# Later unit loads, an earlier parameter step and later state pairs in a one-core recurrent decoder step

## The chip, the core and the metric

The kernel runs on one core of one Trainium2 chip. The metric is device time of one execution in microseconds (us), and the time of a kernel is the median of several executions. TensorE (PE), VectorE (DVE), ScalarE (ACT), GpSimd (POOL) and SyncE (SP) each work through their own queue in order; they wait for one another through semaphores. SP does nothing here but issue transfers from the chip's main memory. ACT and POOL issue a few as well.

## The reference

The program is one inference step of a decoder layer for 256 prompt tokens and 8 samples of 4 tokens (288 columns in all), with width 2048, in float32. What is computed:

- A modulation: `mod = silu(c) @ w_ada + b_ada`, six vectors of 2048 for each of nine conditions. They shift and scale the normed input of both halves of the layer and gate their results.
- `proj = xn @ w_in`, split into the inputs of three branches and three merge gates.
- Branch 1, a linear recurrence (RG-LRU): a causal convolution of width 4, then `r` and `i` as sigmoids of block-diagonal products, `log_a = 8 * r * log_sigmoid(lam)`, `a = exp(log_a)`, `u = sqrt(1 - exp(2 log_a)) * i * x`, and the scan `h = a*h + u`.
- Branch 2, gated linear attention (GLA), and branch 3, mLSTM, both with matrix states that are read, updated and written for each sample.
- `merged = sum over branches of sigmoid(gate) * (y @ w_br)`, then `x + gt1 * (merged @ w_out)`, and an MLP with squared ReLU, a last norm, and all new states.

## The kernel before

**Tiles.** Activations lie feature by feature: 128 features on the partitions, 288 columns along the free axis. Every large product runs through `stream_` (line 183). A block of weights is 512 output columns wide. It comes in granules: a granule is one raw tile of 128 x 1024 (two times 128 rows of the weight matrix), fetched by SP at line 155, halved into a high part on ACT (`hi`, line 164) and a low part on DVE (`lo`, line 171), and used by 24 matmuls of 288 columns (lines 197 to 199: hi times the activations' high and low parts, lo times their high part). There are three buffers each for raw, hi and lo. Four PSUM tiles `mm` hold one block; a block's evacuation by ACT or DVE must free them before the next block uses them.

**Units.** The modulation's weights are cut into units of 1 MB (`first` and `ada`). `load_one` (line 411) has SP issue a unit's transfer (lines 378, 380 and 391), and `visit` (line 416) has PE run its small matmuls (line 341). Units have buffers of their own, taken in turn from the list in `slots`: a number is a large slot that is free at that time, `None` is the ring tile `ag`, `"st"` is a pair of small tiles. A unit's transfer can only be issued once the visit of the buffer's last unit is over.

**Order.** SP's instructions are put out in the order in which the program emits them (SP is scheduled by hand). The other engines' orders are made by a planner, which simulates the program and picks by priority; `issue_after` puts an instruction behind another one on the same engine. `run` (line 252) goes through a block granule by granule. After each granule it does one step of the pattern that `every` set: `L` loads a unit, `V` visits all units that are loaded, `W` and `N` are a small product's load and work, and a dot does nothing. Then it lets each generator in `side` (the recurrence, GLA, mLSTM) take one step, up to its next `yield`, with high priority and behind the granule's last matmul, hi and lo on their engines. Because raw tiles have three buffers, SP is some granules ahead of PE in its order; when it comes to a load whose buffer is not free, all fetches behind it wait too.

**Stages.** The first product runs in stages 0 to 5 as parts of the modulation become known. Stage 5 (line 764) has 12 granules and the pattern `L L WL L . VN . L L . V .`. After its tenth granule the recurrence `lru()` (line 684) starts beside it. Then come two gate blocks of 8 granules (line 811), whose evacuations are a tanh on ACT (line 807) and a product on DVE (line 808), and the merge of branch 1 (line 1132), in which four times 8 granules of gate weights alternate with 4 of `wbl`. `finish(lru_)` (line 1147) drains what is left of the recurrence before the first 4. The later merges run beside GLA and mLSTM.

**The recurrence.** `lru()` first runs `conv` (line 652): transfers and a group of small operations on POOL, then, for each of 8 feature tiles, one ACT and three DVE operations, with six yields. Then it computes its parameters from `lam` (lines 694 to 713: 128 x 8 values, two ACT and some twenty DVE operations), yields, and runs ten steps in which PE makes two small products per tile (line 728) and ACT makes two tanh, a tanh and an Exp of the tile two steps back (lines 722 to 724). Four square roots on ACT follow (line 731), four groups of products on DVE (735 to 737), the scans (747) and the split into high and low parts (523 and 524).

**mLSTM.** The 16 state tiles of 0.5 MB are loaded on POOL (line 1444), read by PE in pairs (line 1461), updated on DVE and stored on POOL (line 1483). `when(n)` (line 1508) gives the step of pair n; the loads and later steps are tied to it.

Of the kernel before, what the change touches and what calls it, by code (L numbers as in the profile page):

```python
# [10 lines left out]
AF = mybir.ActivationFunctionType  # L11
# [42 lines left out]
def trunk(ctx, tc, io):  # L54
    nc = tc.nc
    PSUM = bass.MemoryType.PSUM
    V, S, G, T, Q = nc.vector, nc.scalar, nc.gpsimd, nc.tensor, nc.sync
# [19 lines left out]
    def slot(i, dt=F32):  # L77
        return big.tile([P, 8, N], dt, tag=f"s{i}", name=nm(f"s{i}"))
# [22 lines left out]
    def Pm(n):  # L101
        a, w = POFF[n]
        return par[:, a:a + w]
# [144 lines left out]
    def every(p, skip=0):  # L248

        pace.update(every=p.split(), n=-skip)  # L250
# [37 lines left out]
    a, w = COFF["eye"]  # L288
# [17 lines left out]
    slots = {"ids": (None,), "n": 1}  # L306
# [275 lines left out]
    qk, vv, lx = slot(8), slot(9), slot(2)  # L582
# [66 lines left out]
    pace.update(pins=pace["adds"][-2:-1])  # L649
    run(stream(win, B_LRU + 1, act1, 2, None, keep=kept))  # L650

    def conv(x, y, w, b, state, cout, scr):

        w = w.rearrange("p (k j) -> p k j", k=8)
        f = flat(scr)
        xp = f[:, 0:448].rearrange("p (k b j) -> p k b j", k=8, b=NB)
        acc = f[:, 448:704].rearrange("p (k b t) -> p k b t", k=8, b=NB)
        tmp = f[:, 704:960].rearrange("p (k b t) -> p k b t", k=8, b=NB)
        co = f[:, 960:1176].rearrange("p (k j) -> p k j", k=8)
        G.dma_start(f[:, 1176:1368], io[state])  # L660
        G.tensor_copy(xp[:, :, :, 3:7], smp(x))
        G.tensor_copy(xp[:, :, :, 0:3], f[:, 1176:1368].rearrange("p (k b j) -> p k b j", k=8, b=NB))
        bc = [P, 8, NB, TS]
        for j in range(4):
            wj = w[:, :, j:j + 1].unsqueeze(3).to_broadcast(bc)
            if j == 0:
                G.tensor_tensor(out=acc, in0=xp[:, :, :, 0:4], in1=wj, op=ALU.mult)
                G.tensor_tensor(out=acc, in0=acc, in1=b.unsqueeze(2).unsqueeze(3).to_broadcast(bc), op=ALU.add)
            else:
                G.tensor_tensor(out=tmp, in0=xp[:, :, :, j:j + 4], in1=wj, op=ALU.mult)  # L670
                G.tensor_tensor(out=smp(y) if j == 3 else acc, in0=acc, in1=tmp, op=ALU.add)
        G.tensor_copy(co[:, :, 0:3], x[:, :, NP - 3:NP])
        G.tensor_copy(co[:, :, 3:27].rearrange("p k (b j) -> p k b j", b=NB), xp[:, :, :, 4:7])
        G.dma_start(io[cout], co)
        for m in range(8):
            S.activation(y[:, m, 0:NP], x[:, m, 0:NP], AF.Identity, bias=b[:, m:m + 1], scale=w[:, m, 3:4])
            for j in (2, 1, 0):
                s = 3 - j
                V.scalar_tensor_tensor(y[:, m, s:NP], x[:, m, 0:NP - s], w[:, m, j:j + 1], y[:, m, s:NP], ALU.mult, ALU.add)
            if m not in (0, 3):  # L680
                yield


    def lru():
        wax = slot(3)
        wa = flat(wax)[:, 0:1024].rearrange("p (n d) -> p n d", n=8)
        wx = flat(wax)[:, 1024:2048].rearrange("p (n d) -> p n d", n=8)
        G.dma_start(flat(wax)[:, 0:2048], io["lruw"])
        uc = slot(4)
        yield from conv(lx, uc, Pm("lcw"), Pm("lcb"), "lst", "o_lconv", slot(1))  # L690

        lam = Pm("lam")
        e, s, z, a_ = (sc([P, 8], f"lam{i}", 1) for i in range(4))
        S.activation(e, lam, AF.Abs)
        S.activation(e, e, AF.Exp, scale=-1.0)
        V.tensor_scalar(s, e, 2.0, None, ALU.add)
        V.reciprocal(s, s)
        V.tensor_tensor(out=s, in0=s, in1=e, op=ALU.mult)
        V.tensor_tensor(out=z, in0=s, in1=s, op=ALU.mult)
        V.memset(a_, 1.0 / 19)  # L700
        for n in range(8, -1, -1):
            V.tensor_tensor(out=a_, in0=a_, in1=z, op=ALU.mult)
            V.tensor_scalar(a_, a_, 1.0 / (2 * n + 1), None, ALU.add)
        V.tensor_tensor(out=a_, in0=a_, in1=s, op=ALU.mult)
        ls = sc([P, 8], "lam4", 1)
        V.tensor_scalar(ls, lam, 0.0, None, ALU.min)
        V.scalar_tensor_tensor(ls, a_, -2.0, ls, ALU.mult, ALU.add)
        ls2, ls4 = sc([P, 8], "lam5", 1), sc([P, 8], "lam6", 1)
        V.tensor_scalar(ls2, ls, 2.0, None, ALU.mult)
        V.tensor_scalar(ls4, ls, 4.0, None, ALU.mult)  # L710
        hb = sc([P, 2, 8], "hb", 1)
        V.tensor_scalar(hb[:, 0, :], Pm("ba"), 0.5, None, ALU.mult)
        V.tensor_scalar(hb[:, 1, :], Pm("bx"), 0.5, None, ALU.mult)
        yield
        thr, thi, tt = slot(5), slot(0), slot(1)
        aa = thr
        ps = {}
        for n in range(8 + 2):
            if n >= 2:
                i = n - 2  # L720
                for j, t in ((0, thr), (1, thi)):
                    S.activation(t[:, i, :], ps.pop((i, j))[:, :N], AF.Tanh, bias=hb[:, j, i:i + 1], scale=0.5)
                S.activation(tt[:, i, :], thr[:, i, :], AF.Tanh, bias=ls2[:, i:i + 1], scale=ls2[:, i:i + 1])
                S.activation(aa[:, i, :], thr[:, i, :], AF.Exp, bias=ls4[:, i:i + 1], scale=ls4[:, i:i + 1])
            if n < 8:
                for j, w in ((0, wa), (1, wx)):
                    ps[n, j] = misc()
                    T.matmul(ps[n, j][:, :N], w[:, n, :], uc[:, n, :], start=True, stop=True)  # L728
            yield
        for h in range(4):  # L730
            S.activation(tt[:, 2 * h:2 * h + 2], tt[:, 2 * h:2 * h + 2], AF.Sqrt, scale=-0.25)
        yield
        for h in range(4):
            r = slice(2 * h, 2 * h + 2)
            V.scalar_tensor_tensor(thi[:, r], thi[:, r], 1.0, uc[:, r], ALU.add, ALU.mult)
            V.tensor_tensor(out=thi[:, r], in0=thi[:, r], in1=tt[:, r], op=ALU.mult)
            V.scalar_tensor_tensor(thi[:, r], aa[:, r], 1.0, thi[:, r], ALU.add, ALU.mult)
            yield
        st = sc([P, 8, NB], "lh0", 1)
        V.tensor_tensor(out=st, in0=aa[:, :, NP:N:TS], in1=Pm("h0").rearrange("p (k b) -> p k b", k=8), op=ALU.mult)  # L740
        V.tensor_tensor(out=thi[:, :, NP:N:TS], in0=thi[:, :, NP:N:TS], in1=st, op=ALU.add)
        V.memset(aa[:, :, NP:N:TS], 0.0)
        V.memset(aa[:, :, 0:1], 0.0)
        hh = slot(3)
        for h in range(8):
            r = slice(h * N, (h + 1) * N)
            V.tensor_tensor_scan(flat(hh)[:, r], flat(aa)[:, r], flat(thi)[:, r], 0.0, ALU.mult, ALU.add)
            if h % 2:
                yield
        ho = sc([P, 8, 9], "lho", 1)  # L750
        G.tensor_copy(ho[:, :, 0:1], hh[:, :, NP - 1:NP])
        G.tensor_copy(ho[:, :, 1:9], hh[:, :, NP + 3:N:TS])
        G.dma_start(io["o_lh"], ho)
        ylru.extend([slot(0, F32R), slot(1, F32R)])
        for h in range(4):
            r = slice(2 * h, 2 * h + 2)
            split(ylru[0][:, r], ylru[1][:, r], hh[:, r])
            yield
# [2 lines left out]

    a, w = COFF["eye"]
    for i, turn, p in ((2, (5, 4, 0, 1, 2, 3), "F2LL F1FL 2FLL 1 2 ."), (3, (3, 2, 1, 0, 4, 5), "L L . L LV . L L . LLV . ."),
                       (4, (5, 4, 0, 1, 2, 3), "L L . L LV . L L . LLV . ."), (5, (3, 4, 5, 0, 1, 2), "L L WL L . VN . L L . V .")):
        k0, k1, _ = STAGES[i]
        if i == 5:
            slots.update(ids=(6, 7, 3, None), n=0)
        pace.update(hpins=pace["copies"][-1:])
        lead = begin(i, p)
        if i < 5:  # L770
# [37 lines left out]
            V.scalar_tensor_tensor(sg[:, base + m, :], th, 1.0, p, ALU.add, ALU.mult)  # L808
        return f

    every("L L L L . V . .")
    slots.update(ids=("st", None, 6, 7), n=0)
    run(stream(win, B_GATE, act1, KT, gate_silu(0)))
    run(stream(win, B_GATE + 1, act1, KT, gate_silu(4)))

# [316 lines left out]
    def merge(br, y, w):  # L1132
        for b in range(4):
            if br == 0 and b == 2:
                visit()
                slots.update(ids=(None,), n=0)
                every("L . V . . .")
            if br == 0:
                gt = acc[b // 2][:, 4 * (b % 2):4 * (b % 2) + 4, :]
            elif br == 1:  # L1140
# [28 lines left out]
            run(stream(w, b, lambda k: (y[0][:, k, :], y[1][:, k, :]), 8, ev))  # L1169

    slots.update(ids=(None, 7), n=0)
    every("L L . V . .")
    merge(0, ylru, io["wbl"])
    visit()
    every("")
# [85 lines left out]
    def mlstm():  # L1261
# [34 lines left out]
        for t in range(2):  # L1296
            for q in range(2):
                p = misc()
                for i in range(4):
                    n = 4 * q + i  # L1300
# [6 lines left out]
        for h in range(4):  # L1307
            for e in range(2):
                n = 2 * h + e
# [4 lines left out]
        for h in range(4):  # L1314
            for e in range(2):
                n = 2 * h + e
# [3 lines left out]
        for t in range(2):  # L1320
            for q in range(2):
                p = misc()
                for i in range(4):
                    n = 4 * q + i
                    T.matmul(p[:, i * P:(i + 1) * P], mc[:, n, t * P:(t + 1) * P], bdk[:, n * P:(n + 1) * P], start=True, stop=True)
                for i in range(2):
                    h = 2 * q + i
# [30 lines left out]
        for h in range(4):  # L1358
            for e in range(2):
                n = 2 * h + e  # L1360
# [145 lines left out]
            at.setdefault(s, []).append(lambda: f(*a))  # L1506

        def when(n):
            return 5 + n // 2 * 3 + (n >= 10)

        do(0, part, kp, ks, 0, K_LO)
        do(0, part, vp, vs[:, 0:256], 0, V_LO)
# [53 lines left out]

    visit()
    slots.update(ids=(None, "st", 5), n=0)
    every("L L L . V . .", skip=6)
    merge(2, yml, io["wbm"])  # L1570


# [250 lines left out]
```

## Time and profile before

| | us |
|---|---|
| runs, median of 3 (lowest to highest) | 1957.53 (1956.1 to 1958.71) |
| profiled execution, its own time | 1953.31 |
| span of the profiled execution | 1951.5 |
| PE busy with matmuls | 1923.9 |
| DVE busy | 1035.4 |
| ACT busy | 809.7 |
| POOL busy | 233.8 |

The span goes from the first to the last instruction; 1.81 us of the execution lie around it. PE's busy time counts a stretch as busy when at least one matmul is under way; matmuls overlap, so what counts for the rate is how far apart they start. `A <- B` after an engine and a line means that A waited for B, with the sum of the waits, how many there were, and the longest.

### The profile page before, as it was taken

To read this page: it belongs to the slowest core of one execution; us is meant where nothing else is said; L and a number is where in the kernel's file an instruction comes from. 1 tells how busy PE (TensorE), PEld (TensorE's weight loads), DVE (VectorE), ACT (ScalarE), POOL (GpSimd) and SP (SyncE) were. 2 spreads that over 40 slices of the span, in tenths; PEclk is the share of its full clock that TensorE was granted. 3 is DMA by queue.
4 is the path that set the end of the run, shared out by engine and by line. 5 is a ranking of instruction groups with operands and counts; after the bars stand their busy time and mean duration, and the time that the engine had idled before them with its cause. 6 is when DMAs were issued, how large, how long until landed. Compare 5 with 4: busy or idle time off the path is not lost.

```text
span 1951.5 us, 35926 instructions
## 1 busy us (share of the span) xinstructions
PE 1923.9 (99%) x15068; PEld 1827.7 (94%) x15068; DVE 1035.4 (53%) x1595; ACT 809.7 (41%) x1130; POOL 233.8 (12%) x334
## 2 busy tenths in 40 slices
PE   8999999999999999999999999999999999999997
PEld 6898889999999998899999899999999999999997
DVE  6665746535673456654454564445454445454565
ACT  4333474443554353433333454443334333343433
POOL 0000100011042112000012330000000000000101
PEclk9999999999999999999999999999999999999999
DMA  9997766557443468876788464455444444444452
GB/s 393 380 353 258 270 233 233 195 186 266 156 164 110 141 214 306 279 261 252 281 318 320 171 216 153 159 178 169 163 162 163 162 162 164 167 166 172 160 173 107
DMA packets 110065, 416.42 MB, mean 213 GB/s; under 512 B 11632, under 2 KB 11808, under 8 KB 106192
## 3 DMA queue, kind: packets, MB, share of 16 engines
q1 hardware_dynamic: 100800, 381.55, 54.6%
q0 software_dynamic: 8096, 29.19, 4.2%
q10 hardware_dynamic: 1008, 3.39, 0.5%
q8 instruction: 118, 1.93, 0.4%
q14 instruction: 43, 0.35, 0.1%
HBM read 397.27 MB, written 16.81 MB: 212 GB/s over the span
## 4 chain that ended last, share of the span: by engine, by line
PE 95%; DMA 2%; DVE 1%; issue 1%; ACT 0%; POOL 0%; SPq 0%; DVEq 0%; ACTq 0%; POOLq 0%
PE mm L197 28%; PE mm L199 28%; PE mm L198 28%; PE pa L341 4%; DMA raw<-win 1%; DMA s<-wad 1%; PE px L728 0%; DMA s<-mC 0%; PE px L1006 0%; DMA s<-x 0%; PE px L1477 0%; PE pi L1461 0%; PE px L1391 0%; PE px L128 0%; DVE lo L171 0%
## 5 line engine op out<-in xcount | busy, mean ns | idle before, releaser
L171 DVE TENSOR_TENSOR lo<-raw,hi 128x1024 fp32r<-128x1024 f32 x448 | 549.0, 1228 | 563.4 <-ACT hi L164 543.7
L164 ACT ACTIVATE hi<-raw 128x1024 fp32r<-128x1024 f32 x444 | 470.5, 1060 | 794.0 <-PE mm L198 602.0
L197 PE MATMUL mm<-xh,hi 128*128 128x288 f32 x2528 | 744.6, 299 | 4.4 <-DVE s L808 2.0
L198 PE MATMUL mm<-xl,hi 128*128 128x288 f32 x2528 | 741.3, 296 | 0.0
L199 PE MATMUL mm<-xh,lo 128*128 128x288 f32 x2528 | 725.6, 295 | 0.9 <-DVE lo L171 0.8
L197 PEld LDWEIGHTS mm<-xh,hi 128*128 128x128 f32 x2528 | 471.7, 188 | 25.0 <-issue 11.8
L197 PE MATMUL mm<-s,hi 128*128 128x288 f32 x1664 | 490.7, 297 | 0.0
L198 PE MATMUL mm<-s,hi 128*128 128x288 f32 x1664 | 488.2, 295 | 0.0
L199 PE MATMUL mm<-s,lo 128*128 128x288 f32 x1664 | 476.5, 295 | 0.4 <-DVE lo L171 0.4
L198 PEld LDWEIGHTS mm<-xl,hi 128*128 128x128 f32 x2528 | 474.2, 188 | 1.3
L199 PEld LDWEIGHTS mm<-xh,lo 128*128 128x128 f32 x2528 | 469.0, 188 | 3.1 <-DVE lo L171 1.6
L197 PEld LDWEIGHTS mm<-s,hi 128*128 128x128 f32 x1664 | 311.9, 188 | 5.5 <-issue 4.2
L198 PEld LDWEIGHTS mm<-s,hi 128*128 128x128 f32 x1664 | 312.5, 188 | 0.3
L199 PEld LDWEIGHTS mm<-s,lo 128*128 128x128 f32 x1664 | 308.3, 188 | 0.8 <-DVE lo L171 0.7
L171 DVE TENSOR_TENSOR lo<-s,hi 128x1024 fp32r<-128x1024 f32 x80 | 98.0, 1225 | 113.4 <-ACT hi L164 113.4
L164 ACT ACTIVATE hi<-s 128x1024 fp32r<-128x1024 f32 x80 | 84.9, 1061 | 142.4 <-PE mm L198 141.7
L1651 POOL TENSOR_TENSOR t<-t 128x288 f32<-128x288 f32 x64 | 60.2, 951 | 639.2 <-ACT t L1650 639.2
L603 DVE TENSOR_TENSOR s<-s,mm 128x288 f32<-128x288 f32 x92 | 39.6, 450 | 43.4 <-PE mm L199 42.4
L1667 DVE TENSOR_TENSOR s<-s,mm 128x288 f32<-128x288 f32 x96 | 40.3, 450 | 33.9 <-PE mm L199 32.6
L1163 POOL TENSOR_TENSOR s<-s,t 128x288 f32<-128x288 f32 x32 | 33.5, 1074 | 192.6 <-DVE t L1162 192.6
L341 PE MATMUL pa<-s,silc 128*32 128x64 f32 (+3 forms) x832 | 51.2, 373 | 0.7 <-DMA s<-wad 0.6
L524 DVE TENSOR_TENSOR s<-t,s 128x288 fp32r<-128x288 f32 x64 | 33.8, 568 | 15.5 <-ACT s L523 15.5
(404 smaller groups left out, 1152.7 us busy)
## 6 DMA issues: line engine op xcount, KB each, us to landing
raw<-win SPq DMA_DIRECT2D x188, 512.0 KB, 4.8
raw<-wf SPq DMA_DIRECT2D x176, 512.0 KB, 4.1
s<-wf SPq DMA_DIRECT2D x80, 512.0 KB, 3.6
s<-wada SPq DMA_DIRECT2D x26, 1024.0 KB, 9.5
s<-wad SPq DMA_DIRECT2D x24, 1024.0 KB, 10.2
ag<-wada SPq DMA_DIRECT2D x22, 1024.0 KB, 5.6
raw<-wout SPq DMA_DIRECT2D x32, 512.0 KB, 5.6
st<-wada SPq DMA_DIRECT2D x20, 512.0 KB, 6.6
```

The source lines that it names most:

```text
L164: pace["hi"] = S.activation(hi, raw, AF.Copy)
L171: pace["lo"] = V.tensor_tensor(out=lo[:, r], in0=raw[:, r], in1=hi[:, r].bitcast(F32), op=ALU.subtract)
L197: T.matmul(pss[m][:, :N], hi[:, kk, ms], xh, start=k == k0 and not take, stop=False)
L198: T.matmul(pss[m][:, :N], hi[:, kk, ms], xl, start=False, stop=False)
L199: pace["last"] = T.matmul(pss[m][:, :N], lo[:, kk, ms], xh, start=False, stop=k == kt - 1 and keep is None)
L341: pace["prod"] = T.matmul(ps[32 * j:32 * j + 32, h * w // 4:(h + 1) * w // 4], silu_c(k), v[:, j], start=k == 0 and h == 0, stop=k == KT - ...
L524: pace["mod"] = V.tensor_tensor(out=dst_l[:, r], in0=src[:, r], in1=dst_h[:, r].bitcast(F32), op=ALU.subtract)
L603: pace["adds"].append(V.tensor_tensor(out=dst[:, base + m, :], in0=dst[:, base + m, :], in1=p, op=ALU.add))
L1163: G.tensor_tensor(out=a, in0=a, in1=t, op=ALU.add)
L1651: G.tensor_tensor(out=r, in0=r, in1=r, op=ALU.mult)
L1667: V.tensor_tensor(out=a, in0=a, in1=p, op=ALU.add)
```

## The change

- `conv` gets a flag; with it, it yields once after its operations on POOL and before the first of the eight tiles.
- `lru()` computes its parameters before `conv`, with a yield after the reciprocal, and calls `conv` with the flag. It has one yield more than before ahead of its first gate product.
- The four square roots are issued behind the last Exp on ACT.
- Stage 5 loads its last two units at steps 10 and 11 and not at 7 and 8, into slots 5 and 6 and not 6 and 7, and visits them at step 11 and not 10.
- The gate blocks, both parts of the merge of branch 1 and the merge of branch 3 load one step later; their visits stay. The gate blocks use slot 7 before slot 6.
- The mLSTM pairs 10, 12 and 14 run one step later, with what is tied to them.

```diff
-    def conv(x, y, w, b, state, cout, scr):
+    def conv(x, y, w, b, state, cout, scr, apart=False):
...
         G.dma_start(io[cout], co)
+        if apart:
+            yield
         for m in range(8):
...
         uc = slot(4)
-        yield from conv(lx, uc, Pm("lcw"), Pm("lcb"), "lst", "o_lconv", slot(1))
-
         lam = Pm("lam")
...
         V.reciprocal(s, s)
+        yield
         V.tensor_tensor(out=s, in0=s, in1=e, op=ALU.mult)
...
-        yield
+        yield from conv(lx, uc, Pm("lcw"), Pm("lcb"), "lst", "o_lconv", slot(1), True)
...
-                S.activation(aa[:, i, :], thr[:, i, :], AF.Exp, bias=ls4[:, i:i + 1], scale=ls4[:, i:i + 1])
+                exp = S.activation(aa[:, i, :], thr[:, i, :], AF.Exp, bias=ls4[:, i:i + 1], scale=ls4[:, i:i + 1])
...
-        for h in range(4):
-            S.activation(tt[:, 2 * h:2 * h + 2], tt[:, 2 * h:2 * h + 2], AF.Sqrt, scale=-0.25)
+        with tc.issue_after(exp.ins):
+            for h in range(4):
+                S.activation(tt[:, 2 * h:2 * h + 2], tt[:, 2 * h:2 * h + 2], AF.Sqrt, scale=-0.25)
...
-                       (4, (5, 4, 0, 1, 2, 3), "L L . L LV . L L . LLV . ."), (5, (3, 4, 5, 0, 1, 2), "L L WL L . VN . L L . V .")):
+                       (4, (5, 4, 0, 1, 2, 3), "L L . L LV . L L . LLV . ."), (5, (3, 4, 5, 0, 1, 2), "L L WL L . VN . . . . L LV")):
...
-            slots.update(ids=(6, 7, 3, None), n=0)
+            slots.update(ids=(6, 7, 3, None, 5, 6), n=0)
...
-    every("L L L L . V . .")
-    slots.update(ids=("st", None, 6, 7), n=0)
+    every(". L L L L V . .")
+    slots.update(ids=("st", None, 7, 6), n=0)
...
-                every("L . V . . .")
+                every(". L V . . .")
...
-    every("L L . V . .")
+    every(". L L V . .")
...
-            return 5 + n // 2 * 3 + (n >= 10)
+            return 5 + n // 2 * 3 + 2 * (n >= 10)
...
-    every("L L L . V . .", skip=6)
+    every(". L L L V . .", skip=6)
```

## The prediction

> **What bounds the kernel now.** I read the page first, then PE's waits over the whole span, then the stretches around them, then SP's queue there, and last what ended each wait.
>
> ```profile
> PE 1923.9 (99%) x15068; PEld 1827.7 (94%) x15068; DVE 1035.4 (53%) x1595; ACT 809.7 (41%) x1130; POOL 233.8 (12%) x334
> ```
>
> PE, the matrix engine, is idle for 27.6 us of the span of 1951.5 (1951.5 - 1923.9). Nothing here takes a matmul away, so the most that can be won is some of this idle time. PE's waits say which part:
>
> ```profile
> PE pi L537 <- DVE t L533: 5.9, 1, 5.9
> PE mm L197 <- DVE s L808: 2.0, 1, 2.0
> PE pi L1461 <- DMA s<-mC: 1.8, 1, 1.8
> PE mm L197 <- ACT hi L164: 1.4, 1, 1.4
> PE mm L199 <- DVE lo L171: 1.2, 3, 0.6
> PE mm L197 <- DVE s L603: 0.9, 2, 0.8
> ```
>
> The first is the opening norm, which no edit touches. The others lie where the edits are, except the 0.6 in the 1.2, which is at 80 us. The stretches say how much of PE's time is lost in each (columns: the stretch, its length, then busy us and instructions of PE, PEld, DVE, ACT and POOL, the clock, the share of DMA and GB/s):
>
> ```profile
> 185.00:214.00 29.00, 26.40 (x213) 20.16 (x213) 16.39 (x29) 9.60 (x13) 10.19 (x15) 1.00 0.83 317
> ...
> 277.00:300.00 23.00, 20.96 (x160) 19.51 (x160) 19.67 (x30) 11.42 (x15) 0.00 (x0) 1.00 0.60 226
> ...
> 773.00:800.00 27.00, 25.23 (x208) 21.86 (x207) 15.19 (x35) 9.75 (x14) 4.26 (x8) 1.00 0.88 301
> ```
> ```profile
> 1500.00:1600.00 100.00, 100.00 (x753) 100.00 (x752) 49.03 (x56) 38.12 (x46) 7.55 (x8) 1.00 0.46 160
> ```
>
> The idle of the first three is 2.60 + 2.04 + 1.77 = 6.41 us. The last row is undisturbed streaming: 100 us / 753 matmuls = 0.133 us each, so a granule of 24 matmuls (one raw tile of weights, 0.5 MB) takes 3.19 us. That is the unit in which this change moves things. The clock is 1.00 in all of them and plays no part.
>
> Why PE stands there is seen on SP, which issues units (1 MB each) and raw tiles in one hand-written order:
>
> ```profile
> SPq L380 <- PE pa L341: 34.7, 7, 11.4
> ```
>
> This is the row of SP's waits between 150 and 330 us. SP stood 34.7 us at unit loads whose buffer PE had not yet freed by visiting the unit before. All raw tiles behind such a load wait with it.
>
> **Part A: stage 5, loads moved from steps 7 and 8 to 10 and 11.** The chain of waits and SP's order of time show the cost:
>
> ```profile
> 187.57 12.60 DMA raw<-win
> ```
> ```profile
> 165.53 12.48 SPq L155 DMA_DIRECT2D raw<-win  x4
> 186.10 0.38 SPq L380 DMA_DIRECT2D s<-wada  x1
> 186.59 0.41 SPq L155 DMA_DIRECT2D raw<-win  x1
> 187.04 0.43 SPq L380 DMA_DIRECT2D s<-wada  x1
> ```
>
> The last of four raw tiles went out by 178.0 (165.53 + 12.48). Then SP stood at the step-7 load until 186.10, when PE had visited the units in its buffer, and two units and two raw tiles went out within 1.5 us. The raw tile of 187.57 took 12.60 us to land. Of units the median is 9.5 us from issue to landing (the row gives count, KB of each and that median):
>
> ```profile
> s<-wada SPq DMA_DIRECT2D x26, 1024.0 KB, 9.5
> ```
>
> After the change no load stands between the raw tiles of granules 7 to 10. They go out at the pace at which raw buffers come free, some 3 us apart from 178 on, and land with a granule or more in hand. The step-10 load goes to slot 5, last used stages ago, and the step-11 load to slot 6, freed by the visit before 186.10, so neither blocks. Removed: the waits in 185:214 (1.4 on hi, 0.9 on the sums, and 0.2 on lo, which is the 1.2 without the 0.6 above and the 0.4 of part C), **-2.5 us**. Bounds: -2.6 (all idle of the row) and +0.5. The loss would come because the visit now stands at step 11, right behind its second load. SP runs about three granules (9.6 us) ahead and a unit lands in 9.5 us, so it is just in time; one that takes 12.60 us like that raw tile is 3.0 us late, and 3.0 - 2.5 is the other bound. I take the near end because the visit's own order is free: the planner may set matmuls of the next granule before it.
>
> **Part B: gate blocks and merge, loads one granule later.**
>
> ```profile
> 263.46 0.33 SPq L155 DMA_DIRECT2D raw<-win  x1
> 275.29 0.38 SPq L380 DMA_DIRECT2D ag<-wada  x1
> 275.76 0.42 SPq L155 DMA_DIRECT2D raw<-win  x1
> ```
> ```profile
> 278.82 0.69 ACT L731 ACTIVATE s<-s 128x576 f32<-128x576 f32 x1
> 282.17 1.06 ACT L164 ACTIVATE hi<-raw 128x1024 fp32r<-128x1024 f32 x1 [2.67 <-DMA raw<-win]
> 283.25 1.28 ACT L807 ACT_TABLE_LOAD   x1
> 284.54 1.32 ACT L807 ACTIVATE t<-mm 128x288 f32<-128x288 f32 x4
> ```
>
> Again SP stood 11.5 us (263.8 to 275.29) at a unit load. The raw tile behind it landed at 282.06; its hi sat at the head of ACT's in-order queue for 2.67 us, with the four tanh of the finished gate block behind it, a table load before them, and PE without a PSUM buffer: 2.0 us. With the unit load a granule later the tile goes out before SP's stop, and only the next one is late, which PE needs 3.19 us later. So the hi no longer blocks ACT. That alone would remove all 2.0.
>
> **Part C: the recurrence, one granule later, its roots pinned.** The old order gives ACT four table loads in this stretch, the one at 283.25 above and these three:
>
> ```profile
> 270.21 1.28 ACT L731 ACT_TABLE_LOAD   x1
> 271.50 1.83 ACT L731 ACTIVATE s<-s 128x576 f32<-128x576 f32 x3
> 273.36 1.28 ACT L722 ACT_TABLE_LOAD   x1
> 274.65 0.89 ACT L722 ACTIVATE s<-px,hb 128x288 f32<-128x288 f32 x2
> ...
> 277.52 1.28 ACT L731 ACT_TABLE_LOAD   x1
> ```
>
> Pinning the roots behind the last Exp makes two of them: 2 x 1.28 = 2.56 us of ACT saved, all of it beside PE's work. But lru() now yields after its parameters and once more after conv's preparation, so the gate matmuls start at its ninth step and not its eighth: the last tanh and Exp, which start at 274.65 and end by 277.52, move a granule back and end near 280.7. The roots then take 1.28 + 4 x 0.61 = 3.7 us (1.83 for three), to 284.4, and a table load 1.28 more: the block's tanh would come at 285.7, which is 1.2 later than the 284.54 of now. Or they come before the roots, if the planner puts them there. So the bounds of B and C together at this place are -2.0 (tanh first) and +1.2 (roots first). I take **-1.0 us**, on the gain's side of the middle (-0.4), because evacuations carry high priority and their first tanh is ready before 280.7.
>
> The parameters themselves (some twenty DVE operations of 0.17 us) and conv's 24 operations only trade places; POOL's part of conv and its loads keep their order. Later in the recurrence:
>
> ```profile
> 308.22 1.40 DVE L747 TENSOR_TENSOR_SCAN s<-s,s 128x288 f32<-128x288 f32 x2
> 310.37 2.77 DVE L524 TENSOR_TENSOR s<-s,s 128x576 fp32r<-128x576 f32 x4 [0.75 <-ACT s L523]
> 313.05 2.46 DVE L171 TENSOR_TENSOR lo<-raw,hi 128x1024 fp32r<-128x1024 f32 x2
> ```
> ```profile
> PE mm L199 <- DVE lo L171: 0.4, 1, 0.4
> ```
>
> The last scans, then the split of the result, then the lo that PE wants: 0.4 us of PE's waits between 270 and 320 us. One pair of scans (1.40 us) more falls in this burst after the change, but the raw tile ahead of it no longer stands behind a unit load, so the burst can start earlier by more than that. **-0.4 us**, bounds -0.4 and +1.4.
>
> [...] Here the root starts at 271.50, 1.29 us after the load at 270.21 began, and the tanh 1.29 us after that at 283.25: no drain is seen. [...]
>
> **Part D: mLSTM pairs 10, 12, 14 one granule later.**
>
> ```profile
> 767.84 7.43 DMA s<-mC
> 775.31 1.07 PE pi L1461 x16
> ```
>
> The second state tile of pair 10 was on its way until 775.27 (767.84 + 7.43), and PE stood 1.8 us for it. A granule later PE comes to it at 773.3 + 3.2 = 776.5, behind its landing at 775.27. The loads that follow are tied to the pair before them and move along. The tail (gather, squares, sums) moves one step, but its last results wait for the second output-gate block anyway, and are used a whole block of eight granules after that. **-1.8 us**, bounds -1.8 and 0.
>
> **Part E: the other patterns** (second half of the first merge, third merge): PE has no wait there in the table above, so I take 0; visits and units are as many as before. A visit there that comes to stand at its load would be friction's, next.
>
> **Friction.** All orders but SP's are planned anew from 180 us on, and the planner's new order may open a wait like the 0.6 of lo. One such: **+0.6**, bounds 0 and +2 (the size of the largest now).
>
> **Sum**: -2.5 - 1.0 - 0.4 - 1.8 + 0.6 = -5.1 us. The profiled execution took 1953.31 us (1.81 beyond its span), so one like it comes to 1948.2. The runs' median, 1957.53, lies 4.2 above that execution; against it the forecast is **1952.4 us**.
>
> **Rivals.** (1) The stop in stage 5 only moves: six units at steps 10, 11, 1, 2, 3 and 4 are 6 MB in about seven granules, 22 us, with 3.5 MB of raw tiles. 9.5 MB in 22 us is 430 GB/s, and 185:214 moved 317 at a busy share of 0.83. For: that rate. Against: raw tiles have a lead of three granules to lose first. Part A is then 0: 1954.9.
> (2) The roots stand first and the burst is late: +1.2 by the bound of B and C, and +1.4 by that of the burst. -2.5 + 1.2 + 1.4 - 1.8 + 0.6 = -1.1: 1956.4. For it: the granule that the recurrence loses. Against it: hi, lo and raw tiles all come earlier there.
> (3) The change does not reach the waits, because the planner trades them for others of like size: 1957.5. Against it: SP's order is by hand, and D hangs on one landing.
> (4) Slower: the roots alternate with the gate block's tanh on ACT, since both are ready between 280 and 284. A root between two tanh costs 2 x 1.28 + 0.69 = 3.25 us; three of them 9.75. PE wants a PSUM buffer every 0.8 us from 283 on, so nearly all of it is PE's, and the recurrence's end comes 3 us later, into the burst. -2.5 - 1.8 + 0.6 + 9.8 - 2.0 + 3.0 = +7.1: 1964.6. It decides from the second alternation on (6.5 against the 4.3 of A and D). For it: the old order alternated once, at 273.36. Against it: the pin keeps Exp out, and tanh of evacuations have priority.
>
> **How the numbers follow.** Forecast 0.56, (1) 0.13, (2) 0.13, (3) 0.08, (4) 0.10. A measurement of this kernel tells about 0.2% (3.9 us) from no change. Faster by more: the forecast, 0.56. Within: (1), (2) and (3), 0.34. Slower by more: (4), 0.10. The range runs from 1949.0 (A to D at their best ends and no friction is -6.8, or 1950.7, with 1.7 for the spread of the runs) to 1959.0, which holds (1) to (3) with 1.5 of spread and leaves (4) out.
>
> **What would show it.** In the profile after: no wait of PE on hi or the sums near 200 us; SP's raw tiles from 178 to 190 about 3 us apart, none landing after 12 us; no wait at L808 near 283, or a shorter one; two table loads there and not four; no wait at L1461 on mC. Wrong would be: a new wait at the visit of step 11, table loads between tanh of L807, a wait for y at the first merge, or waits of PE that sum to about what they sum to now.

## The result, and the profile after

The changed kernel takes **1946.66 us** (median of 6 executions, 1945.86 to 1948.79), the kernel before took 1956.23 beside it (6, 1953.1 to 1958.71): a ratio of 0.9952, 95% interval 0.9939 to 0.9965. It is faster by more than the 0.2% that can be told from no change, and by more than was forecast (1952.4): the time lies 2.3 us below the low end of the range.

The two profiled executions differ by less: 1948.79 us (span 1946.7) against 1953.31 (1951.5). The rows by core give the mean granted clock, before and then after:

```profile
core 0: 1951.5 us, clock 0.998
```
```profile
core 0: 1946.7 us, clock 0.997
```

A line of the changed code stands up to two lines below its number in the profile before (L808 is now L810, L1461 is L1463). The page's first row, then PE's waits over the span:

```profile
PE 1923.7 (99%) x15068; PEld 1829.7 (94%) x15068; DVE 1032.8 (53%) x1595; ACT 808.2 (42%) x1128; POOL 242.1 (12%) x334
```
```profile
PE pi L537 <- DVE t L533: 5.7, 1, 5.7
PE pi L1463 <- DMA s<-mC: 1.8, 1, 1.8
PE mm L197 <- ACT s L1146: 1.1, 1, 1.1
PE mm L199 <- DVE lo L171: 0.6, 1, 0.6
```

The waits at hi, the sums and L808 are gone. What is left beside the opening norm are 1.8 us for a state tile, in another place than before, and 1.1 at the gates of the first merge. The stretches of after (length, then busy us of PE, PEld, DVE, ACT, POOL, the clock, DMA share, GB/s):

```profile
185.00:214.00 29.00, 29.00 (x244) 24.05 (x237) 19.86 (x42) 11.39 (x16) 10.12 (x15) 1.00 0.90 329
277.00:300.00 23.00, 22.87 (x173) 21.03 (x172) 20.00 (x34) 7.37 (x9) 0.00 (x0) 1.00 0.63 225
300.00:312.00 12.00, 10.91 (x82) 10.67 (x82) 10.15 (x13) 6.56 (x11) 6.28 (x4) 1.00 0.60 212
773.00:800.00 27.00, 25.22 (x209) 22.41 (x208) 16.63 (x36) 9.47 (x14) 4.28 (x8) 0.99 0.92 323
798.00:806.00 8.00, 7.56 (x54) 6.98 (x55) 3.84 (x10) 2.50 (x3) 0.25 (x1) 0.79 0.69 280
```

PE's idle time of 2.60 in 185:214 is 0, the 2.04 of 277:300 is 0.13; 300:312, without idle time before, has 1.09; 773:800 has 1.78 as before (1.77). The clock is the other thing to see: 0.79 in 798:806, right behind a stop of PE at 796.7. It is 0.50 in 802.0:802.8, and the large products start 0.24 us apart from 800.33 to 802.97 and 0.13 apart from 803.14 on. At half clock for 3.4 of the 8 us (799.6 to 803.0) it would be 1 - 0.5 x 3.4 / 8 = 0.79. By that share such a stretch costs 3.4 x 0.5 = 1.7 us, if nothing else would have held PE up in it. The profile before has none ahead of its last 8 us, in which PE has no product left.

SP's waits between 150 and 330 us, and its order in stage 5:

```profile
SPq L155 <- DVE lo L171: 114.9, 34, 7.7
SPq L380 <- PE pa L341: 16.2, 5, 8.4
```
```profile
165.21 20.90 SPq L155 DMA_DIRECT2D raw<-win  x7
186.20 0.39 SPq L380 DMA_DIRECT2D s<-wada  x1
187.28 0.33 SPq L155 DMA_DIRECT2D raw<-win  x1
187.66 0.61 SPq L380 DMA_DIRECT2D s<-wada  x1
```

At the unit loads of this row SP stands 16.2 us where it stood 34.7, and mostly it waits for the raw buffers themselves. Seven raw tiles go out in 20.9 us with no unit between them. ACT at the end of the recurrence, and at the first merge:

```profile
269.32 0.63 ACT L725 ACTIVATE s<-s,lam 128x288 f32<-128x288 f32 x1
269.95 1.28 ACT L733 ACT_TABLE_LOAD   x1
271.24 2.41 ACT L733 ACTIVATE s<-s 128x576 f32<-128x576 f32 x4
273.67 1.28 ACT L723 ACT_TABLE_LOAD   x1
...
276.31 0.40 ACT L809 ACTIVATE t<-mm 128x288 f32<-128x288 f32 x1
...
304.03 2.41 ACT L523 ACTIVATE s<-s 128x576 fp32r<-128x576 f32 x4 [2.83 <-DVE s L749]
306.35 1.04 ACT L164 ACTIVATE hi<-raw 128x1024 fp32r<-128x1024 f32 x1
307.29 0.99 ACT L1146 ACTIVATE s<-mm 128x288 f32<-128x288 f32 x3
```

Two table loads stand where four did, and the roots end at 273.65, before the gate block's first tanh at 276.31. At 304.03 the split of the recurrence's result and a hi stand ahead of the gates of L1146, for which PE waits 1.1 us.

### The profile page after: what moved, and what is told of

It reads as the page before. It is cut to its first block, busy times and chain, and to the rows that moved or that the text cites. A ratio compares the mean times of both kernels' runs of the same rounds, so it can differ in the third digit from the quotient of the medians.

```text
span 1946.7 us, 35923 instructions
## 1 busy us (share of the span) xinstructions
PE 1923.7 (99%) x15068; PEld 1829.7 (94%) x15068; DVE 1032.8 (53%) x1595; ACT 808.2 (42%) x1128; POOL 242.1 (12%) x334
## 4 chain that ended last, share of the span: by engine, by line
PE 97%; DMA 1%; DVE 1%; ACT 1%; issue 0%; SPq 0%; DVEq 0%; POOL 0%; ACTq 0%; POOLq 0%
PE mm L197 29%; PE mm L199 28%; PE mm L198 28%; PE pa L341 4%; DMA s<-wad 1%; DMA s<-mC 1%; PE px L1479 0%; PE pi L1463 0%; PE px L729 0%; PE px L1008 0%; PE px L1393 0%; PE px L128 0%; PE px L848 0%; PE px L1403 0%; PE mm L234 0%
```

## The experiments

Two theories were weighed. **The stops alone**: the gain is the sum of the waits that went. **The clock as well** (theory K in the expectations): behind a stop of PE of one and a half to three us the clock is halved for 3.4 us in a share of the executions, so a stop that goes takes more with it than its length. "Idle" is PE's wait; every time is a median with the lowest, the highest and the number of executions.

**The kernel before once more** (no edit).

> The kernel before, unchanged, for a second profile and more times. Theory V (the part of the gain beyond the forecast, 9.6 us against 5.1, is made of waits on landings that differ from execution to execution; the first profile of before had few of them): the times spread over 3 us or more, and this profile shows a span other than 1951.5 by 1 us or more, with the difference in PE's waits near 200, 283 or 773 us. Rival F (the profile before was typical, and the change gained something that no wait of before shows): the same waits within 0.3 us each, and times above the profile's by a constant.

1956.35 us (1953.43 to 1959.54, 11), ratio 0.9998 (0.9989 to 1.0007). This profile, unlike the first of the same kernel, has two stretches at half clock. Its waits and two stretches:

```profile
PE mm L197 <- DVE s L808: 1.9, 1, 1.9
PE pi L1461 <- DMA s<-mC: 1.9, 1, 1.9
PE mm L197 <- ACT hi L164: 1.7, 1, 1.7
```
```profile
203.00:207.00 4.00, 4.00 (x21) 4.00 (x20) 4.00 (x7) 1.72 (x4) 2.42 (x3) 0.57 0.83 278
...
776.00:780.00 4.00, 4.00 (x27) 3.58 (x20) 2.65 (x8) 1.83 (x3) 0.82 (x2) 0.58 0.67 254
```

The three stops sum to 5.5 us and not 5.2, each within 0.3 of the first profile's; the clock behind two of them is not the same. So theory V of the expectation fell: the span is 2.1 us longer (1953.6), and the listed waits don't show it. The two stretches did not cost alike. By the start of the same large product (a product into a PSUM tile `mm`), this profile falls from 0.1 to 1.75 us behind the first between 4300 and 4400 products, across the stretch at 776, but across the one at 203 only from 0.1 us ahead to 0.2 behind: the waits on the sums that the first profile has there (0.9) are not in it.

In all 17 profiles the mean clock gives the number of such stretches: none at 0.998, one at 0.997, two (or one of twice the length) at 0.996. Sorted by it, 78 executions of the kernel before, run beside these experiments, give:

| mean clock | executions | median us (lowest to highest) |
|---|---|---|
| 0.998 | 13 | 1953.26 (1952.33 to 1954.10) |
| 0.997 | 31 | 1955.03 (1952.95 to 1957.51) |
| 0.996 | 32 | 1956.41 (1954.64 to 1958.84) |
| 0.995 | 2 | 1957.96 (1957.46 and 1958.45) |

All 78: 1955.57. A stretch at half clock takes 1.7 / 1954 = 0.0009 off the mean clock, about a row of the table, and the rows lie 1.4 to 1.8 us apart. (The 0.002 that even the first row lacks lie behind PE's last product: the first profile of before ends with 7.2 us at half clock, that of after with 7.0.) The execution that was profiled before, 1953.31 at 0.998, is of the first row: one in six.

**Each part undone**, the rest as after. Stage 5 and the gate blocks, with their slots:

```diff
-"L L WL L . VN . . . . L LV"
+"L L WL L . VN . L L . V ."
...
-    every(". L L L L V . .")
+    every("L L L L . V . .")
...
```

> The changed kernel with the loads of stage 5 and of the gate blocks back where they were (pattern, visit, slots); all else as changed. By the prediction's parts A and B 2.5 + 1.0 us come back: 1950.2 against 1946.7 of the changed kernel. Theory V: more comes back, 5 to 8 us (1952 to 1955), and the times spread by over 2 us again. Rival F: 1950 with a spread below 1 us.

1949.22 us (1947.64 to 1949.84, 5): 2.6 above the changed kernel, less than the 3.5 expected. The wait of 1.4 on hi is back near 200 us, with half clock behind it; there is no wait at L810.

```profile
PE mm L197 <- ACT hi L164: 1.4, 1, 1.4
```
```profile
203.00:206.00 3.00, 3.00 (x15) 3.00 (x14) 2.45 (x5) 0.94 (x3) 2.25 (x2) 0.50 0.83 281
```

The patterns of the merges (the first of the three is shown):

```diff
-    every(". L L V . .")
+    every("L L . V . .")
...
```

> The changed kernel with the loads of the merges (branch 1, both parts, and branch 3) back one step. By part B's chain the raw tile behind the first merge's unit load is late again and hi blocks ACT: the wait at L809 near 277 us returns, 2.0 us, so 1948.7 against 1946.7. Theory K (each stop of PE of some 1.6 us or more can bring a stretch of 3.4 us at half clock, which costs 1.7 us more, in some of the executions): 1948.7 to 1950.4, in two groups of times 1.7 us apart, the slower with a granted clock lower by 0.001. If the roots' new place is what removed the wait at 283 us: 1946.7 and no wait there.

1947.13 us (1946.36 to 1950.11, 5). The wait of part B is back, by the first merge's pattern, for the gate blocks' own is as changed here:

```profile
PE mm L197 <- DVE s L810: 1.8, 1, 1.8
```

The time grew by 0.5 only. In this profile the wait at L1146 is 0.2 and not 1.1, and there is no stop at pair 14.

The pairs:

```diff
-            return 5 + n // 2 * 3 + 2 * (n >= 10)
+            return 5 + n // 2 * 3 + (n >= 10)
```

> The changed kernel with mLSTM pairs 10, 12 and 14 back at their old steps. By part D 1.8 us come back: 1948.5, with a wait at L1463 for mC at pair 10. Theory V: the wait depends on the landing, so between 1946.7 and 1949.5, and the profile shows the wait at pair 10 or at none. Rival F: the move did nothing (the changed kernel's profile has the wait of 1.8 at pair 12): 1946.7.

1949.31 us (1948.47 to 1951.26, 5): 2.7 above, with a stop on mC at 768.0, longer than before the change, and a clock of 0.57 from 772 to 776.

```profile
PE pi L1463 <- DMA s<-mC: 3.1, 1, 3.1
```

The recurrence (without the pin, too):

```diff
         uc = slot(4)
+        yield from conv(lx, uc, Pm("lcw"), Pm("lcb"), "lst", "o_lconv", slot(1))
         lam = Pm("lam")
...
         V.reciprocal(s, s)
-        yield
...
-        yield from conv(lx, uc, Pm("lcw"), Pm("lcb"), "lst", "o_lconv", slot(1), True)
+        yield
```

> The changed kernel with the recurrence as before (conv first, no extra yields, roots not pinned); all loads and pairs as changed. By the prediction this edit is a loss that the loads make up for: 1946.7 minus up to 1.2 us, so 1945.5 to 1946.7, with four table loads on ACT near 270 us. If the order of the recurrence is itself part of the gain (its first gate products no longer cut the visit of the gate blocks in pieces, 5.5 us for that visit before and 3.1 after): 1948 to 1949, with the visit near 231 us in pieces again.

1946.66 us (1945.52 to 1947.49, 5), the time of the changed kernel. Yet the profile shows what its order is worth. DVE near 200 us in this kernel, then in the changed one:

```profile
199.71 0.44 DVE L603 TENSOR_TENSOR s<-s,mm 128x288 f32<-128x288 f32 x1
200.07 4.65 DVE L681 SCALAR_TENSOR_TENSOR s<-s,par,s 128x255 f32<-128x255 f32 x6
204.64 0.44 DVE L603 TENSOR_TENSOR s<-s,mm 128x288 f32<-128x288 f32 x1
```
```profile
199.90 0.44 DVE L603 TENSOR_TENSOR s<-s,mm 128x288 f32<-128x288 f32 x1
200.26 0.19 DVE L697 RECIPROCAL lam<-lam 128x8 f32<-128x8 f32 x1
201.66 0.46 DVE L603 TENSOR_TENSOR s<-s,mm 128x288 f32<-128x288 f32 x1 [1.21 <-PE mm L199]
```

With conv first, six of its operations (4.65 us) stand ahead of the sum that frees a PSUM buffer, and PE waits 0.6.

```profile
PE mm L197 <- DVE s L603: 0.6, 1, 0.6
```

After 2400 large products the changed kernel's profile is at 435.94 us, this one at 437.48 and the first of before at 442.24: the change is 1.5 us ahead of it there. It loses that again at the pairs: this profile has no wait on mC, and no stretch at half clock there.

**Pairs 10, 12 and 14 moved.** Two steps earlier than in the changed kernel, and one step later for pairs 12 and 14:

```diff
-            return 5 + n // 2 * 3 + 2 * (n >= 10)
+            return 5 + n // 2 * 3
```
```diff
-            return 5 + n // 2 * 3 + 2 * (n >= 10)
+            return 5 + n // 2 * 3 + 2 * (n >= 10) + (n >= 12)
```

> The changed kernel with mLSTM pairs 10, 12 and 14 one step earlier than before the change, so that PE must stand longer for the state tile: two granules less of lead than in the changed kernel, a stop of about 5 us at pair 10. Without theory K: that stop alone, 1946.7 + 4 to 5 = 1951 to 1952, clock as ever. Theory K: a stretch of half clock behind the stop in most executions: 1952.5 to 1954, granted clock 0.997 or less, and in the profile a stretch below full clock just behind the stop.

> The changed kernel with pairs 12 and 14 one more step later (pair 10 as changed). The changed kernel's profile has a wait of 1.8 us for mC left, at pair 14. A granule more covers it: 1946.7 - 1.8 = 1944.9, with no wait at L1463 and all times in one group. If only the landing moves along with the pair (its load is tied to pair 10, which stays): none should be left; if it moves: 1946.7.

Earlier: 1950.68 us (1948.89 to 1952.19, 11), at a mean clock of 0.998 in two executions, 0.997 in seven, 0.996 in two. The clock is as theory K has it; the time lies below both expectations, since the stop is 3.3 us and not 5. The wait, and two stretches of its profile:

```profile
PE pi L1463 <- DMA s<-mC: 3.3, 1, 3.3
```
```profile
764.00:769.20 5.20, 2.52 (x20) 2.29 (x18) 1.23 (x1) 1.52 (x2) 0.00 (x0) 1.00 1.03 417
769.20:776.00 6.80, 6.22 (x34) 4.94 (x35) 2.76 (x8) 1.43 (x2) 1.59 (x3) 0.50 0.74 280
```

Half clock for 6.8 us, two times 3.4, behind a stop of 3.3. Later: 1946.09 us (1945.20 to 1948.53, 5), 0.6 below the changed kernel and not 1.8. There is no wait on mC in its profile, but the wait at L1146 is 1.7.

**The stop filled.** The early pairs again, with products of a tile of ones ahead of the state tiles' products, which are issued behind them; nothing reads their result.

```diff
+            last = pace["last"]
+            if n == 10:
+                ps = misc()
+                for _ in range(36):
+                    last = T.matmul(ps[:, 0:P], ones, ones, start=True, stop=True)
...
+                        with tc.issue_after(last.ins):
```

> As the one with the pairs early, but ahead of pair 10 PE runs 36 small products of ones (about 0.11 us each, 4.0 us in all) whose result nobody uses, so PE is busy while it would stand. Theory K: no half-clock stretch there, granted clock 0.998 in nearly all executions, and a time not above the one without them (1951 to 1952.5), though 4 us of work were added. Without theory K: the same clock with and without the products, and the time the same or up to 4 us more.

1954.31 us (1953.62 to 1954.72, 11), at 0.998 in ten of the eleven. The expectation mis-sized the fill: a product is two instructions, 72 of them 0.11 us apart, 8.0 us and not 4.0.

```profile
L1462 PE MATMUL px<-ones x72: 273/275/275, 764.7 to 772.7; 128*128 128x128 f32 x72
```
```profile
769.00:776.00 7.00, 7.00 (x68) 6.29 (x67) 1.58 (x6) 0.80 (x2) 1.04 (x2) 1.00 0.90 306
```

So it has no stop and 8.0 us of work in its place: 4.6 more than the gap of 3.4, and the lowest time without the fill, 1948.89, and 4.6 make 1953.5. With 15 products (`range(15)`):

> Pairs 10, 12 and 14 two steps earlier than in the changed kernel, so that PE stands 3.3 us for the second state tile of pair 10, with 15 products of ones (30 instructions, by the earlier run 0.11 us each, 3.3 us) put there instead of 36. They add nothing to the result. The same work waits for the same tile, but PE is busy in the meantime. Theory K: no half-clock stretch behind it, so the clock is 0.998 in nearly all executions and the time that of the undisturbed executions of the kernel without the products, 1948.9 to 1949.7 us, say 1949.3. Rival (the lower clock comes and goes by itself and has nothing to do with PE's stops): the clock is mostly 0.997 as without the products, and the time 1950.7 or more, since the products can only take time.

1951.50 us (1950.92 to 1953.60, 11), at 0.998 in eight of eleven. The clock came out nearly as theory K has it, the time did not: the planner put the products ahead of 14 large ones and not into the gap, so that 3.3 us of fill and a wait of 1.8 were both paid.

```profile
PE pi L1469 <- DMA s<-mC: 1.8, 1, 1.8
```
```profile
769.00:776.00 7.00, 6.69 (x59) 6.11 (x60) 3.46 (x10) 1.99 (x4) 1.60 (x3) 1.00 0.80 245
```

Of the rival (the clock comes and goes by itself) little is left: two of 11 executions at 0.998 with the stop of 3.3, eight with 1.8, ten with none, all of the same state tiles.

**The changed kernel once more, and the recurrence's step.**

> The changed kernel once more, for its spread. Theory K (the clock falls to half for some 3.4 us, which costs 1.7 us, in a share of the executions with a stop of PE of 1.6 us or more): its one such stop is the 1.8 us at the second state tile of pair 14, so the executions fall in two groups, most at a mean clock of 0.998 and 1945.9 to 1946.8 us, the others 1.7 us or more above that at 0.997; none lies where the kernel before lies mostly (1955 to 1959). Against K: the times spread evenly, or the long ones have the clock of the short ones.

1946.73 us (1945.97 to 1948.47, 5). Three of the five are at 0.997, where theory K had most at 0.998, and one of the three (1946.73) is hardly longer than the two at 0.998 (1945.97 and 1946.40): the two groups of times that were expected don't show. Its profile (1948.47) has no wait on mC, the tile of pair 14 having landed 1.35 us before PE came; the wait at L1146 is 2.0, with the stretch at half clock behind it:

```profile
PE mm L197 <- ACT s L1146: 2.0, 1, 2.0
```
```profile
309.00:314.00 5.00, 4.90 (x25) 4.90 (x26) 2.52 (x3) 1.90 (x5) 2.72 (x4) 0.66 0.56 164
```

Without the flag of conv, alone and with pairs 12 and 14 one step later:

```diff
-        yield from conv(lx, uc, Pm("lcw"), Pm("lcb"), "lst", "o_lconv", slot(1), True)
+        yield from conv(lx, uc, Pm("lcw"), Pm("lcb"), "lst", "o_lconv", slot(1))
```

> The changed kernel without the yield behind conv's operations on POOL: the recurrence runs one step of a granule earlier, the parameters stay ahead of conv, the pin of the roots stays. Theory (the wait of 1.1 us at the tanh of the first merge's gates, near 306 us, comes from the split of the recurrence's result standing on ACT ahead of them, because the recurrence ends a granule later): that wait is gone or under 0.4 us; the time is 1945.7 us, 1.0 below the changed kernel. Rival (the burst at 300 to 315 us is set by the raw tiles, not by the recurrence's place): the wait stays within 0.3 us of 1.1, and the time at 1946.7.

> The kernel of the run before, with pairs 12 and 14 one step later still, so that the second state tile of pair 14 has landed when PE comes to it. If the two stops are independent: 1.8 us from pair 14 and 1.0 from the tanh, less what other stops take back (the run with pair 14 moved alone gave 0.6): 1945.0 us, clock 0.998 in all executions. Rival (a stop that is taken away only comes back at the next place): 1946.1 as with pair 14 moved alone.

Alone: 1947.68 us (1946.00 to 1950.55, 5). The wait at L1146 is gone, as the theory of the late split had it, and a wait at L810 has come in its place. The time is not better; the profiled execution is the lowest of the five, so what makes the others longer is not shown.

```profile
PE mm L197 <- DVE s L810: 1.0, 1, 1.0
```

With the later pairs: 1945.89 us (1945.46 to 1946.08, 5), 0.998 in all five. It is the lowest of all, 0.8 us or 0.04% below the changed kernel, which can't be told from it (ratios to before 0.9950, 0.9938 to 0.9963, and 0.9956, 0.9944 to 0.9969).

**Each part alone on the kernel before**, whose 27 executions beside these runs gave 1954.94. The edits are those of the change itself: all patterns and slots; `when`; the lines of `conv` and `lru`.

> The kernel before with the later loads alone (stage 5, gate blocks, merges); recurrence and pairs as before. Of the three stops near 200, 283 and 773 us the first two should go. Undisturbed executions of the kernel before take 1953.4 us; the run with only the recurrence undone stood 4.8 us ahead of it before the pairs: 1948.6, and the stop at 773 brings a half-clock stretch in some 0.6 of the executions, 1.0: 1949.6 us, mean clocks 0.997 and 0.998. Rival (the clock has no part in the difference): 1956.3 - 4.8 = 1951.5.

> The kernel before with pairs 10, 12 and 14 one step later alone. The stop at 773 goes, those at 200 and 283 stay. The stop with what is late behind it is worth 2.2 us by the profile after, and 0.6 stretches at half clock 1.0: 1956.3 - 3.2 = 1953.1 us, mean clock mostly 0.997 and 0.996. Rival (no clock): 1954.1. Rival (a stop at pair 14 takes its place, as in the profile after): 1956.

> The kernel before with the recurrence's edits alone (parameters first, two more yields, roots pinned). By the undo of it in the profiles 1.5 us before the pairs, from conv's operations that no longer stand ahead of the sums near 200 us; the stops at 200, 283 and 773 stay: 1954.8 us with a mean clock mostly of 0.996. Rival (worth nothing, as the times of the undo say): 1956.3. Rival (the recurrence's granule later costs where the loads still stop, as the prediction's bound of 1.2 + 1.4 had it): 1958.

| alone | us (lowest to highest, 11 each) | ratio (95%) | against 1954.94 |
|---|---|---|---|
| loads | 1949.85 (1947.72 to 1951.61) | 0.9974 (0.9965 to 0.9983) | -5.1 |
| pairs | 1952.48 (1951.32 to 1957.14) | 0.9992 (0.9983 to 1.0001) | -2.5 |
| recurrence | 1953.88 (1951.99 to 1955.72) | 0.9995 (0.9986 to 1.0004) | -1.1 |

The three add up to -8.6; all together are 1946.67 - 1954.94 = -8.3. The undone parts gave 2.56 + 0.47 + 2.65 + 0.00 = 5.7; that this is less because one stop takes over from another is my reading. The loads show both terms best. Five executions at 0.998 lie at 1947.72 to 1948.63, five at 0.997 at 1949.85 to 1950.96. The profile is one of the latter (1950.28), with the old stop at the pairs and the clock behind it:

```profile
PE pi L1461 <- DMA s<-mC: 2.1, 1, 2.1
```
```profile
771.00:774.60 3.60, 3.60 (x24) 2.87 (x17) 1.94 (x7) 1.83 (x3) 0.54 (x1) 0.53 0.62 252
```

The pairs alone have the stop at pair 14 too (1.5 us). The recurrence alone keeps the 1.4 on hi and the wait at L810, though its roots are in one batch there: that wait hung on the loads, not on the table loads.

```profile
PE mm L197 <- DVE s L810: 1.8, 1, 1.8
```

## Why the prediction was right or wrong

The direction and the places of the stops were right, the level was not. Of the 5.7 us between forecast and time, 2.0 are the level of the kernel before (1957.53 from three executions, 1955.57 from 78), which is chance. The other 3.8 are two steps:

**"The clock is 1.00 in all of them and plays no part" is the step that failed.** It was read off one execution, of the kind that one in six is. The forecast then kept the 4.2 us between that execution and the median as a constant, while part of it was the cost of the very stops that the sum took away. At a clock of 0.998 the two kernels take 1953.26 and 1946.62 us (13 and 7 executions): 6.6 apart. Over all (78 and 11) they are 1955.57 - 1946.67 = 8.90 apart. The 2.3 between go with the clock. Counted by the mean clock, the kernel before has (31 + 2 x 32 + 3 x 2) / 78 = 1.3 stretches at half clock per execution and the changed one 4 / 11 = 0.4, which by 1.7 us each is 1.6. That is a bound from above, for a stretch near 203 us cost only 0.3. So up to 1.6 of the 2.3 is the half clock itself; whether the rest is longer waits in the same executions is not shown.

**The sum was 5.1 where 6.6 came**, term by term:

- A, -2.5: the waits were read rightly, their worth was not. The idle 2.60 of 185:214 is 0, and SP's order is the one described. But between the starts that follow 1050 and 1500 large products, PE runs 578 products in either kernel, as many of each kind: in 82.4 us before (196.19 to 278.57) and 77.8 after (195.87 to 273.67), 4.6 less. With only the recurrence undone it is 79.8, the 2.6 of A; the other 2.0 are the recurrence's new order. Of these 0.6 is the wait on the sums, which comes back there, 0.5 closer spacing of the large products, and 0.8 closer spacing of the visits' small products. The last two stand in no row of waits, so "the most that can be won is some of this idle time" was too narrow. A wait also counts from the end of a product of 0.29 us, and the next could start 0.13 behind that product's start, so it costs 0.16 more than its row says.
- B and C at the gate block, -1.0: mis-sized. The idle time there fell by 1.9, nearly the bound of -2.0. The cause named (a raw tile behind a unit load, its hi ahead of the tanh) stands. That the roots would end near 284.4 and hold up the tanh does not: the last Exp ended at 269.95 and not near 280.7. I had moved it back by the yields alone. Left out were the two table loads and three roots that stood ahead of it before (270.21 to 274.65, 4.4 us), which the pin puts behind it, and that the products before it came 6.5 us earlier by then (after 1400 large products PE is at 257.68 before and at 251.14 after).
- "The parameters themselves and conv's 24 operations only trade places": this failed. With conv first, its operations stand ahead of the sums, and the recurrence's edits are worth the 2.0 above, 1.5 after 2400 large products, 1.1 as a part alone (an interval that reaches to no change) and nothing in the time when undone alone.
- C's burst, -0.4: the wrong side of its bounds. The lo's 0.4 went, but the split on ACT cost 1.1 or 2.0 at L1146; without conv's flag that is gone or 0.3, and 1.0 at L810 is there.
- D, -1.8: pair 10 came behind its tile as said (no wait at 770.37). With no stop at pair 14 the pairs are worth 2.2 (the profile with the recurrence undone is 4.8 us ahead of the first of before after 2400 large products and 7.0 after 4700). What was missed is what is late next: pair 14's second tile moved along and went out at 787.84, 5.2 us earlier than before, but took 10.55 us to land, at 798.39, where it had taken 3.9. Why it took longer was not tried.

```profile
798.44 1.07 PE L1463 MATMUL pi<-s,s 128*32 128x257 f32 x16 [1.78 <-DMA s<-mC]
```

  In the second profile that stop is not there. D's gain is paid back in some executions and kept in others.
- Friction, +0.6: the right kind, too small. The new stops are those at L1146 and at pair 14, 1.1 and 1.8 us in the first profile after, 2.0 and none in the second.

Rival (4) fell: no root stands between two tanh of the gate block. Rival (1) fell: the visit at step 11 did not wait. Rivals (2) and (3) fell with the time.

What a table load costs was read rightly: the rows of after say the same as those of before, 1.29 us from the load's start at 269.95 to the first root's at 271.24.

## What to carry to other kernels

Before a forecast is set against a median, ask which kind of execution the profile is: if its time lies below all others, look at what the others pay that it doesn't, and whether the edits touch that. A stop of the matrix engine cost its own length here and, in a share of the executions (behind 11 of 21 stops of 1.4 us or more in the profiles), a stretch of 3.4 us or twice that at half clock, so stops can be worth removing beyond their length. Waits are not all that an order costs: compare when both kernels start the same product, not only the rows of waits. When a transfer's user is moved and the transfers behind it are tied to it, work out the landing of the last one too, not only of the first that waited.

## What was not expected of the hardware

The half-clock stretches. They are 3.4 us long or twice that, and in two of the profiles they began 3.0 us (changed kernel, 799.6) and 2.7 us (pairs earlier, 769.2) after the start of a stop; the waits ahead of them were 1.4 us (stage 5 undone) to 3.3 us. They don't come always: the stops of 1.9, 1.9 and 1.7 in the second profile of before brought two, those of 2.0, 1.8 and 1.4 in the first none. In the 17 profiles PE stops 21 times for 1.4 us or more behind the first 100 us. Behind 11 of these stops the clock is halved, behind none of the ten of 0.7 to 1.2 us, and nowhere else until PE's last product. What decides in which execution one comes was not tried.
